# Hybrid decoder step: a state update over 128 rows, one product for all new keys, small loads and cache copies in program order

## The chip, the cores and the metric

The kernel runs on one core of a Trainium2 chip. The metric is the device time of one execution in microseconds (us); lower is better. Three runs of the kernel before gave a median of 3202.14 us (3200.97 to 3202.41). On TensorE's clock the profile prints the granted share: 1.00 is 2.4 GHz and 0.50 is 1.2 GHz.

## What is computed

One step of a one-layer decoder trunk for two groups: a prompt of 2048 tokens, and 8 sample sequences of 8 new tokens each, with a cache of 128 keys and values and a recurrent state. The reference, cut to what matters here:

```python
def layer_forward(x, pos, cache_k, cache_v, conv_state, ssm_state, p, decode):
    proj = rms_norm(x, p['norm_w']) @ p['w_in']
    q, k, v, z_a, z_s, xbc, dt_raw, g = jnp.split(proj, [...], axis=-1)
    if decode:      # k_all, v_all: 128 cached and 8 new positions of each sequence
        o_a, new_k, new_v = window_attention_decode(q, k, v, cache_k, cache_v, p['sinks'])
    else:
        o_a = window_attention_prompt(q, k, v, p['sinks'])
    o_s, new_conv, new_ssm = ssd_branch(xbc, z_s, dt_raw, conv_state, ssm_state, p, chunk)
    merged = jax.nn.sigmoid(g_a) * ((o_a * jax.nn.silu(z_a)) @ p['w_attn_proj']) \
           + jax.nn.sigmoid(g_s) * (o_s @ p['w_ssd_proj'])
    return x + merged @ p['w_out'], new_k, new_v, new_conv, new_ssm

# window_attention_decode returns, beside the attention, the last 128 rows of [cache ; new]
#   (120 cached rows and 8 new ones) as the new window
# ssd_scan:  states = einsum('bclgn,bclgh,bclghp->bcghpn', B, decay_to_end * dt, x)
#            h      = h * chunk_decay + states
```

Everything is f32. Model width 1024, 16 query and 4 key heads of 64, 32 state heads of 64 by 128 in 4 groups.

## The kernel before

Three phases share one core. **T1** (`phase_t1`, line 376) takes the prompt in four blocks of 512 tokens: for each block 256 columns of `w_in` at a time are loaded (`raw`, two buffers, line 154), split into a rounded high part and a rest (`whl`, two buffers, lines 149 to 151: ScalarE casts, VectorE subtracts), and multiplied on TensorE (lines 171 and 195). Each block runs the z_attn tiles (`za_tile`), the keys, the values, the queries and the windowed attention. While a block runs, the next block's `xt` rows are loaded and normed (`prep_h`, line 286). **S** (`phase_s`, line 718) projects x, B, C and z of the recurrent branch and scans the state, four blocks by four groups. **T2** (`phase_t2`, line 1139) does the gates and the output products, block 3 first; the two sample phases, `phase_sa` (attention, line 608) and `phase_ss` (state, line 939), are called inside the first block of T2, and their instructions are interleaved with the products of the prompt.

What sets the order: every DMA of the kernel is issued by one engine, SP, in one queue, and every engine runs its instructions in the order in which they stand. That order is made when the program is built, by a scheduler that takes instructions as soon as its own model of time has them ready, so a load that depends on nothing may be put far ahead of the place where the program text has it.

The places that the change touches:

- `init3` (line 227): loads of small tables for phases S and T2. `sinkS` is 16 loads of 8 times 4 bytes; `Dcol` is two loads, each 64 partitions by 16 elements of 4 bytes that lie 8 bytes apart in memory (line 244 and 246). The text calls `init3` at block 3 of T1 (line 586).
- `phase_sa`, lines 641 to 644: the copies of 120 of 128 cached rows of each sequence to the output windows, one DMA of 960 KB for keys and one for values, from memory to memory.
- `phase_sa`, lines 654 to 690, a loop over the 8 sequences. The probabilities `ss` (128 rows of head and token, 136 positions) are transposed in two pieces, 128 positions (line 679) and 8 (line 680); `po` takes two products per key head: 128 cached values (line 689) and the sequence's own 8 new values `vn` (line 690).
- `phase_ss`, lines 1068 to 1097: the state update `st` of four sequences by two heads. `wxs` holds a rounded part in partitions 0 to 63 and its rest in 64 to 127; `Beh` is the rounded B for all 128 rows, `Bel` the rest of B for the first 64.

```python
PE.matmul(pst_, wxs[:, i * P : (i + 1) * P], Beh, start=True, stop=False)
PE.matmul(pst_, wxs[:64, i * P : (i + 1) * P], Bel, start=False, stop=True)
```

Of the kernel before, what the change touches and what calls it, by code (L numbers as in the profile page):

```python
# [17 lines left out]
P = 128  # L18
# [60 lines left out]
def build(tc, nc, a, o, seq, phases=("T1", "S", "T2"), dbg=None):  # L79
# [146 lines left out]

    def init3(xp, trp):
        rows = xp.tile([P, 2, P], F32, name="rows3", tag="xt")
        SY.dma_start(rows[:96, 0], a["conv_w"][0].rearrange("k (c p) -> (k c) p", p=P))
        SY.dma_start(rows[96:120, 0], a["conv_b"][0].rearrange("(c p) -> c p", p=P))  # L230
        SY.dma_start(rows[:16, 1], a["ssd_norm_w"][0].rearrange("(c p) -> c p", p=P))
        ips = trp.tile([P, 256], F32, name="tr", tag="tr")
        PE.transpose(ips[:, :120], rows[:120, 0], ident[:120, :120])
        PE.transpose(ips[:, 128:144], rows[:16, 1], ident[:16, :16])
        V.tensor_scalar(cwb.rearrange("p k c -> p (k c)"), ips[:, :120], 0.5, None, ALU.mult)
        V.tensor_copy(snw, ips[:, 128:144])
        for h in range(NH):
            SY.dma_start(sinkS[8 * h : 8 * h + 8], a["sinks"][0][h : h + 1].partition_broadcast(8))
        V.tensor_scalar(nsinkS, sinkS, -1.0, None, ALU.mult)
        SY.dma_start(A_bc, a["A_log"][0].partition_broadcast(P))  # L240
        A.activation(A_bc, A_bc, AF.Exp)
        V.tensor_scalar(A_bc, A_bc, -1.0, None, ALU.mult)
        SY.dma_start(dtb_bc, a["dt_bias"][0].partition_broadcast(P))
        dv = a["D_skip"][0].rearrange("(c l) -> l c", l=2)
        for hl in range(2):
            SY.dma_start(Dcol[64 * hl : 64 * hl + 64], dv[hl].partition_broadcast(64))
# [361 lines left out]
    def phase_sa(oas):  # L608
        with ExitStack() as es:
# [43 lines left out]
            po = op.tile([P, 2, 8, 32], F32, name="po", tag="po")  # L653
            for b in range(8):
# [3 lines left out]
                vn = wk.tile([8, 256], F32, name="vn", tag="vn")  # L658
                SY.dma_start(vn, vn_d[8 * b : 8 * b + 8])
# [17 lines left out]
                softmax(wk, s, mx, 136, nsinkS, sinkS, 1)  # L677
                tr = trp.tile([P, 256], F32, name="tr", tag="tr")
                PE.transpose(tr[:, :P], s[:, 0, :P], ident)
                PE.transpose(tr[:8, P:], s[:, 0, P:], ident)  # L680
                PT = wk.tile([P, P], F32, name="PTs", tag="PTs")
                PTn = wk.tile([8, P], F32, name="PTn", tag="PTn")
                A.copy(PT, tr[:, :P])
                A.copy(PTn, tr[:8, P:])
                for pair in range(2):
                    for kvl in range(2):
                        kv = 2 * pair + kvl
                        dst = po[64 * kvl : 64 * kvl + 64, pair, b]
                        PE.matmul(dst, cv[:, kv * HD : (kv + 1) * HD], PT[:, kv * 32 : kv * 32 + 32], start=True, stop=False)
                        PE.matmul(dst, vn[:, kv * HD : (kv + 1) * HD], PTn[:, kv * 32 : kv * 32 + 32], start=False, stop=True)  # L690
# [27 lines left out]
    def phase_s():  # L718
        with ExitStack() as es:
# [219 lines left out]
    def phase_ss(vss):  # L939
        with ExitStack() as es:  # L940
# [44 lines left out]
            for g in range(4):  # L985
# [84 lines left out]
                Bl = wk.tile([64, P], F32, name="Bl", tag="Bl")  # L1070
                V.tensor_tensor(Bl, trb[:64], Bh[:64].bitcast(F32), ALU.subtract)
# [3 lines left out]
                for q in range(2):  # L1075
                    bs = slice(4 * q, 4 * q + 4)
                    Beh = wk.tile([P, 4, P], F32R, name="Beh", tag="a")
                    Bel = wk.tile([64, 4, P], F32R, name="Bel", tag="AB")
                    ohb = ohS[:, bs].unsqueeze(2).to_broadcast([P, 4, P])
                    G.tensor_tensor(Beh, Bh.bitcast(F32).unsqueeze(1).to_broadcast([P, 4, P]), ohb, ALU.mult)  # L1080
                    G.tensor_tensor(Bel, Bl.unsqueeze(1).to_broadcast([64, 4, P]), ohb[:64], ALU.mult)
                    for i in range(4):
# [11 lines left out]
                        PE.matmul(pst_, wxs[:64, i * P : (i + 1) * P], Bel, start=False, stop=True)  # L1094
# [234 lines left out]
```

## Time and profile before

| | before |
|---|---|
| median of 3 runs | 3202.14 us (3200.97 to 3202.41) |
| the profiled execution's own time | 3201.39 us |
| its span, first to last instruction | 3199.6 us |
| TensorE products (PE) busy | 3085.4 us, 96% |
| VectorE (DVE) | 2081.5 us, 65% |
| ScalarE (ACT) | 1419.9 us, 44% |
| GpSimd (POOL) | 982.5 us, 31% |
| mean granted TensorE clock | 0.989 |

The profile is one execution, its times are us from the span's start. PE is the products, PEld the loading of weights that runs beside them. A line such as L195 is a line of the kernel before. In rows of single instructions the columns are start, duration, engine and line, operation, output<-inputs, count, and in brackets the idle time of that engine just before, with what ended it. SPq is the SP queue: its duration is how long the issue of a DMA held SP. f32 products are carried out in two passes and show as two instructions; f32r ones (`fp32r` operands) in one.

### The profile page before, as it was taken

How to read it: one execution, taken by the hardware profiler on the slowest of the kernel's cores; microseconds unless marked ns; L12 is line 12 of the kernel's file. 1: busy time of each engine (PE TensorE's matmuls, PEld its weight loads, DVE VectorE, ACT ScalarE, POOL GpSimd, SP SyncE). 2: the span in 40 equal slices, each digit the busy share in tenths (PEclk: the TensorE clock that was granted, in tenths of full speed). 3: DMA queues.
4: the chain of work that ended last, by engine and by line, in shares of the span. 5: the costliest groups of instructions: out<-in, count | busy, mean ns of one | idle time of the engine just before them, and what ended most of it. 6: DMA issues, size and time to landing. Idle time of an engine off the chain costs nothing.

```text
span 3199.6 us, 49248 instructions
## 1 busy us (share of the span) xinstructions
PE 3085.4 (96%) x19038; PEld 2649.2 (83%) x19038; DVE 2081.5 (65%) x3265; ACT 1419.9 (44%) x2786; POOL 982.5 (31%) x905
## 2 busy tenths in 40 slices
PE   6999999998999999999999998999999999999999
PEld 5978787877899877777777776787877799999888
DVE  3877868787777787888878886455555554334433
ACT  3544535455555555555656564333233333222321
POOL 1523232231445555555656664000121100000000
PEclk8999999999999999999999998999999999999999
DMA  6544425333433544444454444445655564345443
GB/s 215 157 141 117 141 76 180 108 107 103 126 121 119 172 130 124 154 148 131 129 167 147 129 141 128 139 131 154 205 181 143 155 206 132 99 132 175 137 107 103
DMA packets 472931, 448.88 MB, mean 140 GB/s; under 512 B 33824, under 2 KB 420664, under 8 KB 472648
## 3 DMA queue, kind: packets, MB, share of 16 engines
q1 hardware_dynamic: 472696, 445.73, 45.2%
q8 instruction: 150, 2.46, 0.3%
q14 instruction: 85, 0.70, 0.1%
HBM read 382.39 MB, written 65.35 MB: 140 GB/s over the span
## 4 chain that ended last, share of the span: by engine, by line
PE 73%; DVE 12%; DMA 5%; POOL 5%; issue 3%; ACT 2%; SPq 0%; POOLq 0%; DVEq 0%; ACTq 0%
PE mm L184 46%; PE mm L195 12%; PE mm L171 5%; DVE acc L760 3%; DVE whl L151 2%; POOL L L857 2%; DMA raw<-in_w_in_dram 2%; PE sc L522 1%; PE tr L551 1%; POOL ws L881 1%; DVE zs L897 1%; PE tr L539 1%; PE st L884 1%; DMA xt<-in_x_prompt_dram 1%; ACT whl L150 1%
## 5 line engine op out<-in xcount | busy, mean ns | idle before, releaser
L184 PE MATMUL mm<-hT,whl 128*128 128x512 f32 (+1 forms) x6720 | 1349.1, 357 | 10.4 <-DMA hT<-h_d 4.1
L184 PEld LDWEIGHTS mm<-hT,whl 128*128 128x128 f32 x6720 | 1119.5, 190 | 181.1 <-issue 12.6
L151 DVE TENSOR_TENSOR whl<-raw,whl 128x2048 fp32r<-128x2048 f32 (+1 forms) x232 | 524.6, 2265 | 280.4 <-ACT whl L150 273.0
L184 PE MATMUL mm<-ot,whl 128*128 128x512 f32 (+1 forms) x2880 | 569.1, 355 | 2.8 <-DVE whl L151 2.5
L184 PEld LDWEIGHTS mm<-ot,whl 128*128 128x128 f32 x2880 | 474.2, 188 | 74.9 <-issue 5.7
L150 ACT CAST whl<-raw 128x2048 fp32r<-128x2048 f32 (+1 forms) x232 | 412.7, 1786 | 263.3 <-PE mm L184 132.5
L195 PE MATMUL mm<-whl,hT 128*128 128x256 f32 (+1 forms) x2304 | 307.8, 289 | 23.7 <-DVE zs L421 17.2
L195 PEld LDWEIGHTS mm<-whl,hT 128*128 128x128 f32 x2304 | 290.7, 192 | 28.2 <-DVE zs L421 17.9
L760 DVE SCALAR_TENSOR_TENSOR acc<-cr,cwb,acc 128x512 f32<-128x512 f32 x288 | 284.5, 990 | 15.8 <-ACT acc L755 7.0
L857 POOL TENSOR_TENSOR L<-L,cbm 128x1024 f32<-128x1024 f32 x64 | 182.5, 2861 | 94.4 <-DVE cbm L846 92.8
L195 PE MATMUL mm<-whl,ot 128*128 128x256 f32 (+1 forms) x1632 | 203.9, 285 | 0.0
L195 PEld LDWEIGHTS mm<-whl,ot 128*128 128x128 f32 (+1 forms) x1632 | 197.6, 188 | 5.3 <-issue 4.9
L171 PE MATMUL mm<-hT,whl 128*128 128x512 f32 x768 | 194.3, 403 | 2.3 <-ACT hT L277 2.1
L855 ACT ACTIVATE L<-AB,acs 128x128 f32<-128x128 f32 x512 | 157.0, 389 | 38.6 <-PE py L878 29.0
L171 PEld LDWEIGHTS mm<-hT,whl 128*128 128x128 f32 x768 | 142.8, 192 | 33.8 <-ACT hT L277 2.5
L368 ACT ACTIVATE s<-s,ng 128x128 f32<-128x128 f32 x256 | 99.9, 393 | 94.4 <-DVE ng L362 84.2
L150 ACT CAST ot<-v 128x512 fp32r<-128x512 f32 x96 | 58.9, 620 | 162.1 <-DVE v L1195 86.9
L881 POOL TENSOR_TENSOR ws<-wx,ws 128x512 fp32r<-128x512 f32 x64 | 112.2, 1752 | 10.1 <-ACT ws L880 9.8
L374 POOL TENSOR_SCALAR s<-s,den 128x128 f32<-128x128 f32 x128 | 50.1, 403 | 202.7 <-DVE den L370 140.6
L826 ACT ACTIVATE th<-mm 128x512 f32<-128x512 f32 (+1 forms) x80 | 40.0, 509 | 160.8 <-PE mm L184 153.6
L764 ACT ACTIVATE th<-acc 128x512 f32<-128x512 f32 x96 | 60.5, 630 | 111.8 <-DVE acc L760 111.7
L1187 ACT ACTIVATE t<-mm 128x512 f32<-128x512 f32 (+1 forms) x76 | 37.6, 518 | 162.4 <-PE mm L184 141.9
(318 smaller groups left out, 3912.5 us busy)
## 6 DMA issues: line engine op xcount, KB each, us to landing
raw<-in_w_in_dram SPq DMA_DIRECT2D x120, 1024.0 KB
hT<-h_d SPq DMA_DIRECT2D x80, 512.0 KB
raw<-in_w_in_dram SPq DMA_DIRECT2D x64, 512.0 KB
AB<-ac_d SPq DMA_DIRECT2D x64, 512.0 KB
raw<-in_w_ssd_proj_dram SPq DMA_DIRECT2D x32, 1024.0 KB
v_d<-zs SPq DMA_DIRECT2D x16, 1024.0 KB
v<-v_d SPq DMA_DIRECT2D x64, 256.0 KB
raw<-in_w_attn_proj_dram SPq DMA_DIRECT2D x64, 256.0 KB
```

What stands on the lines that cost most here:

```text
L150: A.copy(hi, src)
L151: V.tensor_tensor(lo, src, hi.bitcast(F32), ALU.subtract)
L171: PE.matmul(ps, hl[:, x, k, c0 : c0 + P], ht[:, y, :], start=first and i == 0, stop=last and i == n - 1,)
L184: PE.matmul(ps, hl[:, x, k, c0 : c0 + P], ht[:, y, lo : lo + n], start=i == 0, stop=i == 3 * len(hT) - 1,)
L195: PE.matmul(ps, ht[:, x, tt * P : tt * P + m], hl[:, y, k, :n], start=i == 0, stop=i == 3 * len(hT) - 1,)
L368: A.activation(s[:, i, :width], s[:, i, :width], AF.Exp, bias=ng[:, i : i + 1], accum_out=den[:, i : i + 1])
L374: G.tensor_scalar(s[:, i, :width], s[:, i, :width], den[:, i : i + 1], 0.5, ALU.mult, ALU.mult)
L760: V.scalar_tensor_tensor(out=acc, in0=raw[:, k : k + TB], scalar=cwb[:, k, ct : ct + 1], in1=acc, op0=ALU.mult, op1=ALU.add)
L764: A.activation(th, acc, AF.Tanh)
L855: A.activation(L[:, h], AB[:, h], AF.Relu, scale=-1.0, bias=acs[:, hc.start + h : hc.start + h + 1])
L857: G.tensor_tensor(L, L, cbm[:, c].unsqueeze(1).to_broadcast([P, 8, P]), ALU.mult)
L881: G.tensor_tensor(ws[:, 1], wx, ws[:, 0].bitcast(F32), ALU.subtract)
```

## The change

1. `init3`'s loads go through `late`, which pins them to their place in the program's order on SP: after all that the text has before them.
2. The cache copies leave `phase_sa`. They become 16 copies of one sequence each (120 KB), two after every second group of phase S, pinned as well.
3. In `phase_sa` the new values of all sequences are loaded once (`vn`, 64 rows). Each sequence's 8 columns of new probabilities are put into a zeroed tile `new` (128 by 64) on POOL and transposed to 64 rows; `PTn` collects them. The product per sequence and key head is only that with the cache; four products of 64 rows by 256 columns at the end do the new values of all sequences, and are added to a copy of `po`.
4. In `phase_ss` the rest of B (`Bl`) is padded with zeros to 128 rows, `Bel` too, and the second state product runs over 128 rows.

```diff
+    def late(dst, src):
+        tc.keep_in_program_order(SY.dma_start(dst, src))
+
     def init3(xp, trp):
-        SY.dma_start(rows[:96, 0], a["conv_w"][0].rearrange("k (c p) -> (k c) p", p=P))
+        late(rows[:96, 0], a["conv_w"][0].rearrange("k (c p) -> (k c) p", p=P))
...
         for h in range(NH):
-            SY.dma_start(sinkS[8 * h : 8 * h + 8], a["sinks"][0][h : h + 1].partition_broadcast(8))
+            late(sinkS[8 * h : 8 * h + 8], a["sinks"][0][h : h + 1].partition_broadcast(8))
...
-            SY.dma_start(Dcol[64 * hl : 64 * hl + 64], dv[hl].partition_broadcast(64))
+            late(Dcol[64 * hl : 64 * hl + 64], dv[hl].partition_broadcast(64))
...
-                SY.dma_start(ow[:, 0:120], a[f"cache_{nm}"][0].rearrange("b j h d -> b j (h d)")[:, 8:P])
                 SY.dma_start(ow[:, 120:P], scr.rearrange("(b t) c -> b t c", b=8))
...
+            vn = one.tile([64, 256], F32, name="vn")
+            SY.dma_start(vn, vn_d)
+            PTn = one.tile([64, NKV, 8, 32], F32, name="PTn")
             for b in range(8):
...
-                vn = wk.tile([8, 256], F32, name="vn", tag="vn")
-                SY.dma_start(vn, vn_d[8 * b : 8 * b + 8])
...
+                new = wk.tile([P, 64], F32, name="new", tag="new")
+                G.memset(new, 0.0)
+                G.tensor_copy(new[:, 8 * b : 8 * b + 8], s[:, 0, P:136])
                 PE.transpose(tr[:, :P], s[:, 0, :P], ident)
-                PE.transpose(tr[:8, P:], s[:, 0, P:], ident)
+                PE.transpose(tr[:64, P:], new, ident)
...
-                A.copy(PTn, tr[:8, P:])
+                A.copy(PTn[:, :, b], tr[:64, P:].rearrange("p (v q) -> p v q", v=NKV))
...
-                        PE.matmul(dst, cv[:, kv * HD : (kv + 1) * HD], PT[:, kv * 32 : kv * 32 + 32], start=True, stop=False)
-                        PE.matmul(dst, vn[:, kv * HD : (kv + 1) * HD], PTn[:, kv * 32 : kv * 32 + 32], start=False, stop=True)
+                        PE.matmul(dst, cv[:, kv * HD : (kv + 1) * HD], PT[:, kv * 32 : kv * 32 + 32], start=True, stop=True)
+            pon = one.tile([P, 2, 8, 32], F32, name="pon")
+            A.copy(pon, po)
+            pn = op.tile([P, 2, 8, 32], F32, name="po", tag="po")
+            for pair in range(2):
+                for kvl in range(2):
+                    kv = 2 * pair + kvl
+                    PE.matmul(
+                        pn[64 * kvl : 64 * kvl + 64, pair].rearrange("p b q -> p (b q)"), vn[:, kv * HD : (kv + 1) * HD],
+                        PTn[:, kv].rearrange("p b q -> p (b q)"), start=True, stop=True,
+                    )
+            V.tensor_tensor(pon, pn, pon, ALU.add)
+            po = pon
...
                     stats(b, g)
+                    for nm in ("k", "v"):
+                        for r in range((4 * b + g) * 8 // (4 * NB), (4 * b + g + 1) * 8 // (4 * NB)):
+                            late(o[f"{nm}_win_s"][r, 0:120], a[f"cache_{nm}"][0, r, 8:P].rearrange("j h d -> j (h d)"))
...
-                Bl = wk.tile([64, P], F32, name="Bl", tag="Bl")
-                V.tensor_tensor(Bl, trb[:64], Bh[:64].bitcast(F32), ALU.subtract)
+                Bl = wk.tile([P, P], F32, name="Bl", tag="Bl")
+                G.memset(Bl[64:], 0.0)
+                V.tensor_tensor(Bl[:64], trb[:64], Bh[:64].bitcast(F32), ALU.subtract)
...
-                    Bel = wk.tile([64, 4, P], F32R, name="Bel", tag="AB")
+                    Bel = wk.tile([P, 4, P], F32R, name="Bel", tag="AB")
...
-                        PE.matmul(pst_, wxs[:64, i * P : (i + 1) * P], Bel, start=False, stop=True)
+                        PE.matmul(pst_, wxs[:, i * P : (i + 1) * P], Bel, start=False, stop=True)
```

How the change moves instructions is read from the built programs. In the rows below a line number belongs to its own program (the changed kernel's lines are 3 to 20 further down), then comes the operation, output<-inputs and the size of the output, and xN for N in a row.

SP, block 0 of T1, before, from the last stores of the first block's `hT` on (`xt` is the next block's input, `raw` the next weights, `out_dram` the output windows):

```order
L282 DMA h_d_1_61<-hT 128x1024
L238 DMA sinkS<-in_sinks_dram 8x1
L240 DMA A_bc<-in_A_log_dram 128x32
L282 DMA h_d_1_61<-hT 128x1024
L243 DMA dtb_bc<-in_dt_bias_dram 128x32
L246 DMA Dcol<-in_D_skip_dram 64x16x1 x2
L290 DMA xt<-in_x_prompt_dram 128x1024
L282 DMA h_d_1_61<-hT 128x1024
L290 DMA xt<-in_x_prompt_dram 128x1024
L643 DMA out_dram<-in_cache_k_dram 8x2x15360
L282 DMA h_d_1_61<-hT 128x1024
L643 DMA out_dram<-in_cache_v_dram 8x2x15360
```

The same stretch after:

```order
L285 DMA h_d_0_60<-hT 128x1024
L577 DMA tab_2442<-in_rope_p_dram 128x4x80
L285 DMA h_d_1_61<-hT 128x1024 x2
L293 DMA xt<-in_x_prompt_dram 128x1024 x2
L285 DMA h_d_1_61<-hT 128x1024 x2
L157 DMA raw<-in_w_in_dram 128x8x256 x3
L476 DMA dt_d_112<-dtt 128x128
```

All loads of `init3` and both cache copies are gone from between the stores and the loads of `xt` and `raw`.

SP, block 3 of T1, after (before, `dt_d` followed the store of `oa_d` directly; L228 is the line of `late`):

```order
L157 DMA raw<-in_w_in_dram 128x8x256
L566 DMA oa_d_1_73<-zs 128x4x128
L228 DMA rows_6540<-in_conv_w_dram 96x128
L228 DMA rows_6540<-in_conv_b_dram 24x128
L228 DMA rows_6540<-in_ssd_norm_w_dram 16x128
L228 DMA sinkS<-in_sinks_dram 8x1 x16
L228 DMA A_bc<-in_A_log_dram 128x32
L228 DMA dtb_bc<-in_dt_bias_dram 128x32
L228 DMA Dcol<-in_D_skip_dram 64x16x1 x2
L476 DMA dt_d_115<-dtt 128x128
L157 DMA raw<-in_w_in_dram 128x8x128 x6
```

The 23 small loads now stand here, ahead of the weights of the last z_attn tiles.

PE, second sequence of `phase_sa`, before (`mm` are products of the prompt):

```order
L679 MATMUL tr<-cst,ss 128x128
L680 MATMUL tr<-cst,ss 8x128
L663 MATMUL tr<-cst,ck 64x128 x4
L184 MATMUL mm<-ot,whl 128x512 x2
L184 MATMUL mm<-hT,whl 128x512 x17
L689 MATMUL po<-PTs,cv 64x32
L690 MATMUL po<-PTn,vn 64x32
L689 MATMUL po<-PTs,cv 64x32
L690 MATMUL po<-PTn,vn 64x32
L689 MATMUL po<-PTs,cv 64x32
L690 MATMUL po<-PTn,vn 64x32
```

and after:

```order
L685 MATMUL tr<-cst,ss 128x128
L686 MATMUL tr<-cst,new 64x128
L666 MATMUL tr<-cst,ck 64x128 x4
L184 MATMUL mm<-ot,whl 128x512 x2
L184 MATMUL mm<-hT,whl 128x512 x17
L694 MATMUL po<-PTs,cv 64x32 x4
L673 MATMUL sc<-KC,QS 32x128
```

The transposes and the products of the prompt stand as before; the products of 8 rows between those of 128 are gone. In `phase_ss` all 32 products with `Beh` and 32 with `Bel` are still there, and the phase stands later among the prompt's products: its last one (`st<-ones,sq`) has 86 products of 256 columns and 96 of 288 behind it before the first that reads the sample's result, where it had 220 and 96.

## Rows read from the trace of the kernel before

**Rows 1.** The page's table of engines: busy us, share of the span, instructions.

```profile
PE 3085.4 (96%) x19038; PEld 2649.2 (83%) x19038; DVE 2081.5 (65%) x3265; ACT 1419.9 (44%) x2786; POOL 982.5 (31%) x905
```

**Rows 2.** Windows: stretch, us, busy of PE, PEld, DVE, ACT, POOL; PEclk; DMA share; GB/s.

```profile
40.00:60.00 20.00, 9.13 (x62) 8.00 (x60) 3.04 (x4) 0.23 (x1) 0.00 (x0) 0.88 0.14 37
...
60.00:80.00 20.00, 13.66 (x87) 13.66 (x88) 9.94 (x12) 7.49 (x11) 6.58 (x10) 0.69 0.79 303
...
80.00:100.00 20.00, 18.48 (x150) 18.24 (x149) 10.74 (x16) 6.90 (x11) 10.13 (x9) 1.00 0.36 116
...
640.00:660.00 20.00, 20.00 (x172) 20.00 (x170) 15.62 (x29) 9.18 (x22) 9.40 (x9) 1.00 0.29 75
...
2050.00:2100.00 50.00, 50.00 (x269) 41.01 (x268) 29.47 (x54) 17.06 (x28) 0.60 (x1) 1.00 0.45 148
...
2250.00:2300.00 50.00, 47.79 (x371) 42.36 (x370) 23.52 (x51) 13.00 (x17) 11.49 (x8) 1.00 0.74 225
```

**Rows 3.** Timeline, block 0 of T1: SP, ACT, DVE and PE around the long stall.

```profile
40.59 1.44 SPq L246 DMA_DIRECT2D Dcol<-in_D_skip_dram  x2
...
42.13 3.15 SPq L290 DMA_DIRECT2D xt<-in_x_prompt_dram  x1
...
63.94 1.06 ACT L251 ACTIVATE junk<-xt 128x1024 bf16<-128x1024 f32 x1 [20.95 <-DMA xt<-in_x_prompt_dram]
...
65.60 0.69 DVE L421 SCALAR_TENSOR_TENSOR zs<-th,mm 128x512 f32<-128x512 f32 x1 [21.27 <-ACT th L420]
...
66.34 14.12 PE L195 MATMUL mm<-whl,hT 128*128 128x256 f32 x89 [16.10 <-DVE zs L421]
```

**Rows 4.** DMA view of 40 to 62 us, and a 2 us window inside it.

```profile
DMA packets 2620, 1.02 MB, mean 46 GB/s; under 512 B 2383, under 2 KB 2383, under 8 KB 2620
...
56.00:58.00 2.00, 0.00 (x0) 0.00 (x0) 0.00 (x0) 0.00 (x0) 0.00 (x0) 0.50 0.05 0
```

**Rows 5.** Timeline, block 3 of T1: SP, ACT and PE where the small loads now stand.

```profile
619.45 0.32 PE L233 MATMUL tr<-cst,rows 120*128 120x120 f32 x1
...
621.71 0.38 SPq L563 DMA_DIRECT2D oa_d<-zs  x1
...
636.63 1.00 SPq L157 DMA_DIRECT2D raw<-in_w_in_dram  x2
...
659.32 1.99 ACT L150 CAST whl<-raw 128x1024 fp32r<-128x1024 f32 x2
```

**Rows 6.** Timeline, DVE and PE: sample attention, and other products of 64 columns of weights.

```profile
617.58 1.94 PE L551 MATMUL tr<-PT,vT 128*64 128x512 f32 x8
...
2103.05 0.30 PE L689 MATMUL po<-PTs,cv 128*64 128x32 f32 x2
...
2104.88 0.44 PE L670 MATMUL sc<-KC,QS 64*32 64x128 f32 x8
...
2107.02 0.29 DVE L372 TENSOR_SCALAR ss<-ss,den 128x136 f32<-128x136 f32 x1
...
2112.05 0.27 PE L679 MATMUL tr<-cst,ss 128*128 128x128 f32 x1
```

**Rows 7.** Timeline, PE in `phase_ss`: the two state products and what follows them.

```profile
2246.43 0.39 PE L1093 MATMUL st<-Beh,wxs 128*128 128x512 f32 x1
...
2246.75 0.50 PE L1094 MATMUL st<-Bel,wxs 64*128 64x512 f32 x1
...
2247.18 0.51 PE L195 MATMUL mm<-whl,ot 128*128 128x256 f32 x2
...
2265.91 0.39 PE L1093 MATMUL st<-Beh,wxs 128*128 128x512 f32 x1
...
2266.13 1.00 PE L195 MATMUL mm<-whl,ot 128*128 128x256 f32 x7
```

**Rows 8.** Timeline, PE and DVE at the end of `phase_ss`.

```profile
2592.29 0.63 PE L1127 MATMUL st<-ones,sq 128*64 128x1 f32 x8
...
2600.07 2.23 DVE L1137 TENSOR_TENSOR vss<-vss,rb 128x256 f32<-128x256 f32 x4 [3.02 <-DMA rb<-rss_d]
```

More of the change, by code (lines that the diff above doesn't have):

```diff
@@ L225, in init2 @@
         V.tensor_scalar(wrow[:, 0], wrow[:, 0], 0.125, None, ALU.mult)
+    def late(dst, src):
+        tc.keep_in_program_order(SY.dma_start(dst, src))
     def init3(xp, trp):
         rows = xp.tile([P, 2, P], F32, name="rows3", tag="xt")
-        SY.dma_start(rows[:96, 0], a["conv_w"][0].rearrange("k (c p) -> (k c) p", p=P))
-        SY.dma_start(rows[96:120, 0], a["conv_b"][0].rearrange("(c p) -> c p", p=P))
-        SY.dma_start(rows[:16, 1], a["ssd_norm_w"][0].rearrange("(c p) -> c p", p=P))
+        late(rows[:96, 0], a["conv_w"][0].rearrange("k (c p) -> (k c) p", p=P))
+        late(rows[96:120, 0], a["conv_b"][0].rearrange("(c p) -> c p", p=P))
+        late(rows[:16, 1], a["ssd_norm_w"][0].rearrange("(c p) -> c p", p=P))
         ips = trp.tile([P, 256], F32, name="tr", tag="tr")
@@ L237, in init3 @@
         for h in range(NH):
-            SY.dma_start(sinkS[8 * h : 8 * h + 8], a["sinks"][0][h : h + 1].partition_broadcast(8))
+            late(sinkS[8 * h : 8 * h + 8], a["sinks"][0][h : h + 1].partition_broadcast(8))
         V.tensor_scalar(nsinkS, sinkS, -1.0, None, ALU.mult)
-        SY.dma_start(A_bc, a["A_log"][0].partition_broadcast(P))
+        late(A_bc, a["A_log"][0].partition_broadcast(P))
         A.activation(A_bc, A_bc, AF.Exp)
         V.tensor_scalar(A_bc, A_bc, -1.0, None, ALU.mult)
-        SY.dma_start(dtb_bc, a["dt_bias"][0].partition_broadcast(P))
+        late(dtb_bc, a["dt_bias"][0].partition_broadcast(P))
         dv = a["D_skip"][0].rearrange("(c l) -> l c", l=2)
         for hl in range(2):
-            SY.dma_start(Dcol[64 * hl : 64 * hl + 64], dv[hl].partition_broadcast(64))
+            late(Dcol[64 * hl : 64 * hl + 64], dv[hl].partition_broadcast(64))
     def norm_x(xt, jp, nwb, n=P):
@@ L677, in phase_sa @@
                 softmax(wk, s, mx, 136, nsinkS, sinkS, 1)
+                new = wk.tile([P, 64], F32, name="new", tag="new")
+                G.memset(new, 0.0)
+                G.tensor_copy(new[:, 8 * b : 8 * b + 8], s[:, 0, P:136])
                 tr = trp.tile([P, 256], F32, name="tr", tag="tr")
                 PE.transpose(tr[:, :P], s[:, 0, :P], ident)
-                PE.transpose(tr[:8, P:], s[:, 0, P:], ident)
+                PE.transpose(tr[:64, P:], new, ident)
                 PT = wk.tile([P, P], F32, name="PTs", tag="PTs")
-                PTn = wk.tile([8, P], F32, name="PTn", tag="PTn")
                 A.copy(PT, tr[:, :P])
-                A.copy(PTn, tr[:8, P:])
+                A.copy(PTn[:, :, b], tr[:64, P:].rearrange("p (v q) -> p v q", v=NKV))
                 for pair in range(2):
@@ L1077, in phase_ss @@
                     Beh = wk.tile([P, 4, P], F32R, name="Beh", tag="a")
-                    Bel = wk.tile([64, 4, P], F32R, name="Bel", tag="AB")
+                    Bel = wk.tile([P, 4, P], F32R, name="Bel", tag="AB")
                     ohb = ohS[:, bs].unsqueeze(2).to_broadcast([P, 4, P])
                     G.tensor_tensor(Beh, Bh.bitcast(F32).unsqueeze(1).to_broadcast([P, 4, P]), ohb, ALU.mult)
-                    G.tensor_tensor(Bel, Bl.unsqueeze(1).to_broadcast([64, 4, P]), ohb[:64], ALU.mult)
+                    G.tensor_tensor(Bel, Bl.unsqueeze(1).to_broadcast([P, 4, P]), ohb, ALU.mult)
                     for i in range(4):
```

## Prediction

> **What bounds the kernel now.** I read the page's table of engines first. TensorE is busy for 96% of the span, the others for 65% and less [rows 1]. So an edit pays in one of two ways only: it closes one of TensorE's few gaps, or it makes TensorE's own work shorter. The gaps are 114 us in all (span 3199.6 less 3085.4). The windows show where the largest is: from 40 to 100 us PE is idle for 10.87, 6.34 and 1.52 us, together 18.7 us, while 2050 to 2100 has no gap and 2250 to 2300 only 2.2 us [rows 2].
>
> The timeline of 40 to 100 us then says what ended that gap; the reader should follow it backwards. PE waited 16.10 us for the VectorE step on `zs`, which had waited 21.27 us for ScalarE's `th`; ScalarE runs in order and stood at the `junk` of the next block's norm, 20.95 us, for the DMA of `xt` [rows 3]. On SP, the issue of `xt` at 42.13 stands directly behind the two `Dcol` loads, issued at 40.59. What those loads cost is in the DMA view: of the 2620 packets between 40 and 62 us, 2383 are under 512 B, and 2 x 64 x 16 = 2048 of these are `Dcol`'s single elements. In a window inside the stall the DMA share is 0.05, less than one of 16 engines (0.06), at 0 GB/s [rows 4]: one engine works through tiny packets and all else in the queue waits. The wait of ScalarE ends when `xt` lands, 63.94; 42 us to there, less some 2 us for `xt` itself, leaves about 19 us as the length of that stretch, an estimate.
>
> The gap has a second price. The granted clock at 56 to 58 is 0.50, which is the 1.2 GHz level [rows 4], and the mean of 60 to 80 is 0.69 [rows 2]. With only 0.50 and 1.00 in play, 0.5x + 1.0(20 - x) = 0.69 x 20 gives x = 12.4: half clock until about 72.4. PE worked from 66.34 [rows 3], so it ran 6.1 us at half clock, where 3.0 us would have done.
>
> **The change, part by part.** The sum is made against the profiled execution, 3201.39 us; the median of the runs is 0.75 us above it, which I neglect.
>
> *A, loads leave block 0.* The rows of the order on SP show `xt` and `raw` with neither the small loads nor the cache copies ahead. What goes is the wait of 16.1 us and 3.0 us of half clock: **-19.1**. Late next are the `xt` rows and the `raw` weights themselves; with 1.97 MB of copies gone too, which ran at 303 GB/s [rows 2], there is less ahead of them than there was. Bounds: -14 if a new short wait for `xt` stays, -21.7 if the other 2.6 us of gaps in this stretch go too.
>
> *B, sample attention.* Per sequence the 16 passes of `po` run from 2103.05 to 2104.88: 1.83 us, 0.115 each [rows 6]. Half of them are dropped. The nearest row for what is left are the small products of `sc`, which follow each other without a change of rows: 0.44 for 8, 0.055 each [rows 6]; at 0.115 each nothing is saved by ending the alternation itself. I take 0.08, about midway, for each of 8 passes, so 0.64 in place of 1.83, or 1.2 a sequence, 9.6 over eight. Against that stand four products of 64 rows and 256 columns in two passes each, 8 passes. Products of 512 columns take 1.94 for 8 [rows 6], so half, 0.12, for 256: 1.0, and 0.3 for going in and out: **-8.3** (bounds -5.8, with 0.115 kept, and -9.8, with 0.055). The wider transposes of `new` have the same 128 columns to pass and are taken at nothing. POOL's memset and copy come between the softmax's last VectorE step (2107.02, 0.29 long) and the transpose at 2112.05: 4.7 us of room [rows 6]. If they took longer than that, PE would wait in each sequence; the nearest rows are on other engines, so I leave up to 4 us for it in the range.
>
> *C, state update.* The pair of products starts at 2246.43, the 64-row one at 2246.75, the next work at 2247.18: 0.75 us. The 128-row one alone took 0.22 (2265.91 to 2266.13) [rows 7]. So rows changing from 128 to 64 and back costs 0.3 in a pair. Two equal products should take 0.44 to 0.46; I take 0.29 saved, 32 times: **-9.3**, since PE is all but full there (47.79 of 50 [rows 2]) and nothing else takes up the time. Here a rule speaks against the edit. What the rows say is that the pair with 64 rows costs 0.30 us more than two products of 128 rows would. The Trainium skill, in "TensorE: Matmul & The Clock Gate", section "Why this matters for your kernels", has for products over few rows: "K=32 single mm = same time as K=128". By that alone the padding saves nothing and the term is 0, a rival below; this trace does not agree for the mixed pair. Bounds: 0 and -10.
>
> *D, the small loads in block 3.* The order places all 23 behind the store of `oa_d`, issued at 621.71, and ahead of the weights, `raw` x2, issued at 636.63 [rows 5]. The issues take some 0.37 each (`oa_d` 0.38 [rows 5]), 8.5 us, so `Dcol` starts at 630 to 632 on before's clock and holds the one DMA engine for 19 us, to 651 at the latest; with 2 to 4 us of their own the weights land by 655. The cast that needs them ran at 659.32 [rows 5]: 4 to 6 us of room. I cost this at **0**; the cover is the queries and attention of block 3, and without it the stall of A is paid again: up to 19 and 3. `rows` are needed for transposes that ran at 619.45 [rows 5] and now stand 80 products later (some 10 us), by when these short loads are in.
>
> *E, cache copies in phase S.* 16 issues of 0.38 on SP, hidden as SP is not what PE waits for there; 960 KB each for keys and values spread over more than 1000 us. **0** (0 to +5, if loads of S wait behind them).
>
> *F, fillings on POOL and ScalarE.* The memsets of 64 rows, the copy of `po` and the add at the end: POOL is busy 31%, ScalarE 44% [rows 1]. **0** (0 to +3).
>
> *G, the end of the sample's state.* After its last product, at 2592.29, the phase has a chain through DRAM that ends with VectorE's `vss` at 2600.07 and 2.23 [rows 8]: 10 us. Now 86 products of 256 columns at some 0.12 and 96 of 288 at 0.135 (by columns) cover it, 23 us. **0** (0 to +4).
>
> Sum: -19.1 - 8.3 - 9.3 = -36.7, and 3201.4 - 36.7 = 3164.7. I forecast **3165**.
>
> **The rivals.** *The stall only moves.* In block 3 the weights land after ScalarE wants them. For it: the same loads in the same form stand ahead of weights again, and 4 to 6 us of room is thin against a stretch of 19. Against it: from 640 to 660 PE was busy for all of 20 us [rows 2], so weights were in no short supply there. It costs 5 to 15 us (a late cast, partly covered by what PE has queued); with 10 the time is 3175. Chance 0.17.
>
> *Padding buys nothing.* The product of 64 rows is slow for its place, not for its rows: then C is 0 and the time 3174. The rows speak against it: `Beh` alone is followed after 0.22, in the pair after 0.32. Chance 0.06.
>
> *Slower: the state update starves PE.* The phase now stands later among the prompt's products, with fewer left between, and its `st` pairs need copies `Bel` of twice the rows from POOL. If POOL or the loads of the state come too late, PE waits at each pair. The other parts gain 27.4 (A and B), so slower than before begins at 27.4/32 = 0.86 us of wait beyond the 0.75 of before, 1.6 us a pair, and over the bound of 0.2% (6.4 us, about what a measurement of this kernel tells from no change) at 1.06. With 1.2 us of wait a pair: 3201.4 - 27.4 + 38.4 = 3212. For it speaks that the 2.2 us of gaps of 2250 to 2300 lie in this phase [rows 2]; against it, that POOL is busy for 11.49 of those 50 us [rows 2]. Chance 0.03.
>
> That the loads are not moved at all is excluded by the order on SP.
>
> **How the numbers follow.** My forecast has 0.74; the three rivals have 0.17, 0.06 and 0.03. Its own bounds add up as A -14 to -21.7, B -4 (with POOL late -1.8) to -9.8, C -8 to -10, and up to 8 from E, F and G; not all fall the same way, so with all gains at their high ends the time is 3160, and I go 8 further, to 3152, for what moves that I did not cost; the high end of the forecast alone is 3175. The first two rivals reach to 3185 if they come with small losses; **3152 to 3182** takes in most of both and leaves out less than 2 in 10. Faster by over 0.2%: 0.95; within 0.2%: 0.02 (a stall in block 3 of the full length with C at 0); slower: 0.03.
>
> **What would show it.** Right: from 40 to 72 us no half clock and no wait over 2 us; a stretch with the DMA share at 0.05 at about 612 to 631 (block 3 starts earlier by A) with PE busy through it; eight passes of `po` in a row in well under 1 us; `st` pairs 0.45 apart. Wrong: a wait of PE or ScalarE for `raw` in block 3 (D), pairs still at 0.75 (C), a wait of the new transposes for POOL (B), gaps of PE between 2200 and 2650 that were not there, or a wait for `rb` before the third block of the output products (G). The prediction as a whole falls if the half clock appears anywhere it had not been: 3 us then for every 6 us of work.

## The result, and the profile after

The changed kernel takes 3165.31 us in the median of four runs (3161.97 to 3170.36) against 3202.27 us before (four runs, 3200.97 to 3208.05): ratio 0.9882, 95% interval [0.9864, 0.9901], 38 us less (32 to 44). Forecast were 3165, with 3152 to 3182 around it. As the parts below show, that the middle was hit so closely is partly luck: two gains were larger than forecast, and a loss that had been put at nothing took the surplus back, and in the profiled execution more than that.

The profiled execution is the slowest of the four, 3170.36 us with a span of 3168.2; against [rows 1] PE's busy time fell by 21.4 us and the span by 31.4, so some 10 us of idle time went too. The page's table of engines after:

```profile
PE 3064.0 (97%) x18982; PEld 2638.7 (83%) x18982; DVE 2082.5 (66%) x3266; ACT 1421.1 (45%) x2787; POOL 977.8 (31%) x925
```

The windows after, with the columns of [rows 2]: block 0, then the place of the small loads in block 3, then the end of block 3.

```profile
40.00:60.00 20.00, 20.00 (x153) 19.39 (x152) 13.25 (x16) 8.43 (x12) 7.76 (x10) 1.00 0.43 146
60.00:80.00 20.00, 20.00 (x166) 20.00 (x164) 9.56 (x16) 5.78 (x9) 7.50 (x9) 1.00 0.34 109
80.00:100.00 20.00, 20.00 (x173) 20.00 (x171) 15.94 (x31) 10.47 (x20) 8.20 (x9) 1.00 0.21 56
...
610.00:620.00 10.00, 10.00 (x87) 10.00 (x86) 6.54 (x11) 3.89 (x7) 6.52 (x7) 1.00 0.05 4
620.00:630.00 10.00, 10.00 (x87) 10.00 (x87) 7.20 (x12) 5.25 (x8) 6.62 (x7) 1.00 0.05 0
690.00:700.00 10.00, 1.82 (x6) 0.98 (x8) 8.06 (x16) 5.21 (x17) 0.72 (x2) 0.69 1.01 365
```

PE has no gap left from 40 to 100 us, and its clock stays at 1.00, where [rows 2] had 18.7 us idle and 0.88 and 0.69. The stretch with the DMA share of 0.05 is back at 610 to 630, and PE works through it. But 690 to 700 has 8.2 us of idle time, which stood nowhere in the sum. Half clock is not new there: before, the same place had 4.7 us of idle time and a clock of 0.71:

```profile
710.00:720.00 10.00, 5.28 (x29) 4.23 (x26) 9.80 (x17) 5.61 (x14) 3.13 (x2) 0.71 1.02 378
```

The timeline of ACT, DVE and PE there (duration of a row of several is that of all):

```profile
689.00 3.70 ACT L150 CAST whl<-raw 128x2048 fp32r<-128x2048 f32 x2
...
692.74 0.40 ACT L371 ACTIVATE s<-s,ng 128x128 f32<-128x128 f32 x1
...
690.93 4.49 DVE L151 TENSOR_TENSOR whl<-raw,whl 128x2048 fp32r<-128x2048 f32 x2 [0.16 <-ACT whl L150]
...
695.74 0.16 DVE L372 TENSOR_TENSOR den<-den,es 128x4 f32<-128x4 f32 x1
...
696.43 0.61 DVE L375 TENSOR_SCALAR s<-s,den 128x128 f32<-128x128 f32 x2
...
696.86 1.13 PE L542 MATMUL tr<-cst,s 128*128 128x128 f32 x4 [8.30 <-DVE s L375]
```

PE needs the scaled probabilities `s`. Their exps (L371) wait on ScalarE behind two casts of phase S's first weights, 3.7 us, and the scaling waits on VectorE behind the two subtracts of the same weights, 4.5 us. No DMA ends any of these waits. In the order of the program before, ScalarE takes these casts after the exps of that softmax:

```
before:  L368 ACTIVATE s,den<-s,ng 128x128 x3
         L365 ACTIVATE es<-es 128x4
         L368 ACTIVATE s,den<-s,ng 128x128
         L420 ACTIVATE th<-mm 128x512
         L150 CAST hT<-hs 128x64 x2
         L150 CAST whl<-raw 128x2048 x2
after:   L423 ACTIVATE th<-mm 128x512
         L150 CAST hT<-hs 128x64 x2
         L150 CAST whl<-raw 128x2048 x2
         L150 CAST hT<-hs 128x64
         L371 ACTIVATE s,den<-s,ng 128x128 x4
```

That this is built into the order, by a pin on loads of tables, the prediction had not looked for. Before, the same place had a wait of its own, from the same subtracts, but a shorter one:

```profile
716.68 1.12 PE L496 MATMUL tr<-cst,qr 128*128 128x128 f32 x4 [4.72 <-DVE qr L351]
```

The sample phases after, PE's timeline:

```profile
2101.44 0.43 PE L694 MATMUL po<-PTs,cv 128*64 128x32 f32 x8
2101.80 0.44 PE L673 MATMUL sc<-KC,QS 64*32 64x128 f32 x8
...
2170.88 1.08 PE L701 MATMUL po<-PTn,vn 64*64 64x256 f32 x8
2171.89 0.96 PE L184 MATMUL mm<-ot,whl 128*128 128x512 f32 x3
...
2243.83 0.39 PE L1113 MATMUL st<-Beh,wxs 128*128 128x512 f32 x1
2244.06 0.39 PE L1114 MATMUL st<-Bel,wxs 128*128 128x512 f32 x1
2244.29 0.52 PE L195 MATMUL mm<-whl,ot 128*128 128x256 f32 x3
```

Eight passes of `po` take 0.36 us (2101.44 to 2101.80) where 16 took 1.83 [rows 6]; the end product of all sequences takes 1.01 us (2170.88 to 2171.89); the `st` pair takes 0.46 us where it took 0.75 [rows 7]. PE's waits there from 2190 to 2640, by what ended them (total, times, longest), do not name `rb`, `Bel` or POOL; the first is a load of the state (the last row below is the same wait before):

```profile
PE tr L1108 <- DMA h<-in_state_ssm_dram: 4.1, 3, 2.2
PE st L1113 <- DVE h L1116: 1.4, 1, 1.4
...
PE tr L1088 <- DMA h<-in_state_ssm_dram: 0.9, 1, 0.9
```

To see where the time went, the traces are laid side by side at five products that come in every version: the product a sixteenth of the way through T1's `mm<-whl,hT` (83.35 us before), one at 13 sixteenths of it (609.71, early in block 3), the middle one of phase S's `py` (1445.58), T2's first `mm<-ot,whl` (2012.29) and its last `mm<-whl,ot` (3196.14). The table has the change in each stretch against before, from one profiled execution each.

| | block 0 | to block 3 | end of T1 and half of S | rest of S | T2 | all |
|---|---|---|---|---|---|---|
| the change | -22.0 | +0.9 | +10.9 | -1.4 | -19.9 | -31.5 |
| the change again (e5) | -22.4 | -0.5 | +8.7 | +1.5 | -18.4 | -31.0 |
| e1, pinned loads only | -20.1 | -1.7 | +8.0 | +0.5 | +4.5 | -8.9 |
| e2, products only | +0.2 | +2.0 | +3.1 | +0.8 | -8.4 | -2.3 |
| e3, padding only | +1.6 | -0.1 | +2.4 | -1.7 | -9.2 | -7.1 |
| e4, D in 128 packets only | -16.8 | -2.0 | +0.5 | +1.6 | +0.7 | -15.9 |
| e6, change, D in 128 packets | -21.9 | +2.7 | +9.1 | +1.5 | -24.0 | -32.6 |
| e7, change, casts held | -22.8 | -2.3 | +8.9 | +1.8 | -21.1 | -35.4 |
| e8, loads not pinned, D in 128 | -18.7 | +3.1 | -0.7 | +3.8 | -20.3 | -32.9 |
| e9, copies only | -2.6 | 0.0 | +1.2 | -1.1 | +4.1 | +1.5 |
| e10, e6 and e7 together | -22.5 | -2.1 | +2.7 | +2.2 | -14.5 | -34.2 |
| e11, e8 and a later hold | -19.7 | -0.6 | +2.8 | +0.9 | -22.2 | -38.8 |
| e12, D loaded twice | +19.3 | -0.3 | -1.4 | +1.9 | -2.8 | +16.8 |

The second column, where the programs do nearly the same, shows the scatter of one execution: some 3 us to either side. T2 scatters more: the four versions that leave its work alone (e1, e4, e9, e12) have -2.8 to +4.5 there. Runs of one kernel differ by up to 14 us (before, 3199 to 3213 over all chips), so a term of 2 or 3 us is not told from the totals.

### The profile page after: what moved, and what is told of

The parts are those of the page before. It is cut to its first block, busy times and chain, and to the rows that moved or that the text cites. A ratio compares the mean times of both kernels' runs of the same rounds, so it can differ in the third digit from the quotient of the medians.

```text
span 3168.2 us, 49176 instructions
## 1 busy us (share of the span) xinstructions
PE 3064.0 (97%) x18982; PEld 2638.7 (83%) x18982; DVE 2082.5 (66%) x3266; ACT 1421.1 (45%) x2787; POOL 977.8 (31%) x925
## 4 chain that ended last, share of the span: by engine, by line
PE 73%; DVE 13%; POOL 5%; DMA 4%; issue 3%; ACT 2%; SPq 0%; POOLq 0%; DVEq 0%; ACTq 0%
PE mm L184 46%; PE mm L195 12%; PE mm L171 5%; DVE acc L776 3%; DVE whl L151 2%; POOL L L873 2%; PE tr L554 2%; PE sc L525 1%; POOL ws L897 1%; DVE zs L913 1%; PE tr L542 1%; DMA raw<-in_w_in_dram 1%; PE st L900 1%; PE py L894 1%; DMA v<-v_d 1%
## 5 line engine op out<-in xcount | busy, mean ns | idle before, releaser
L371 ACT ACTIVATE s<-s,ng 128x128 f32<-128x128 f32 x256 | 99.9, 393 | 88.4 <-DVE ng L365 81.2
L1215 DVE SCALAR_TENSOR_TENSOR v<-v,snw,rb 128x512 f32<-128x512 f32 x64 | 48.1, 767 | 96.0 <-DMA v<-v_d 95.6
```

Source lines behind the costliest of these rows:

```text
L371: A.activation(s[:, i, :width], s[:, i, :width], AF.Exp, bias=ng[:, i : i + 1], accum_out=den[:, i : i + 1])
```

## The experiments

The first four take the change apart.

**e1, the pinned loads alone**, part 1 of the diff: `init3` uses `late`; the cache copies and all products are before's.

> Only part 1: the loads of init3 are pinned, the cache copies stay in phase_sa, products as before. Theory: this part alone gives -22 us in block 0 (stall and half clock gone) and gives back about 10 us at the end of block 3, where its built order, as that of the change, puts casts of phase S's first hT and whl ahead of the last exps of a softmax that PE waits for: about 3202 - 22 + 10 = 3190 us, with a wait of some 8 us at about 690. Rival: the give-back comes from the 16 cache copies in phase S or from the products, then 3180. Second rival: the cache copies, which here still stand ahead of xt in block 0, hold the stall up, then less than 16 of the 22 us are gained.

Measured: 3191.66 us, ratio 0.9956 [0.9941, 0.9970], 14 us less. Block 0 gains 20.1, with 2.3 us of short waits left where the changed kernel has none, and the end of T1 loses 8.0. Its wait there is the same to a hundredth:

```profile
695.50 1.13 PE L542 MATMUL tr<-cst,s 128*128 128x128 f32 x4 [8.30 <-DVE s L375]
```

So the loss belongs to the pinned loads, not to the copies or the products; both rivals fall.

**e2, the products of the sample attention alone**, the diff's lines in `phase_sa` without the copies.

> Only part 3: the new keys of all sequences in one product per key head. Theory: 8 passes of po in 0.36 us in place of 16 in 1.83, eight times (-11.8), and 1.0 us for the end products: -10.8, so 3191 us. Rival: the copies and the add at the end, or the new order of the products, give some of it back: 3194 to 3198. The stall of block 0 stays.

Measured: 3197.41 us, ratio 0.9974 [0.9965, 0.9983], 8 us less (5 to 11). In its trace each sequence takes 0.36 us for `po` as in the changed kernel, which is worth 8 x 1.48 = 11.8 less 1.0; T2 as a whole is 8.4 us shorter. The missing 2.4 lie within the scatter of a stretch, so whether something is given back stays open.

**e3, the padding alone**, part 4 of the diff.

> Only part 4: the second state product over 128 rows. PE's order is the same as before's, so the term stands alone. Theory: a change between 64 and 128 rows costs PE 0.29 us in a pair, 32 pairs: -9.3, so 3193 us, pairs at 0.46 us. Rival: waits for POOL's wider Bel take it back, then pairs with waits ahead and 3198 to 3202.

Measured: 3195.22 us, ratio 0.9969 [0.9957, 0.9981], 10 us less (6 to 14); T2 is 9.2 us shorter, the forecast of 32 x 0.29, though T2 scatters by more than the two agree. The pairs themselves, with the order of PE unchanged:

```profile
2248.40 0.39 PE L1094 MATMUL st<-Beh,wxs 128*128 128x512 f32 x1
2248.63 0.39 PE L1095 MATMUL st<-Bel,wxs 128*128 128x512 f32 x1
2248.86 0.40 PE L195 MATMUL mm<-whl,ot 128*128 128x256 f32 x2
```

The product over 128 rows does twice the work of the one over 64 and takes 0.23 us where that took 0.43 [rows 7]. The rival that padding buys nothing, and the rule of the Trainium skill behind it ("TensorE: Matmul & The Clock Gate", "Why this matters for your kernels"), do not hold where products over 64 and 128 rows take turns. Its page "TensorEngine Tiling (Array Packing)", section "Key Properties", says that a change of tiling mode drains TensorE; the 0.29 us of a pair fit that, but no run here shows that it is the cause.

**e4, what made the stall.** The kernel before, with every load and copy still in block 0, but D comes in the order of memory.

```diff
...
-        dv = a["D_skip"][0].rearrange("(c l) -> l c", l=2)
+        SY.dma_start(Drow.rearrange("p c l -> p (c l)"), a["D_skip"][0].partition_broadcast(P))
         for hl in range(2):
-            SY.dma_start(Dcol[64 * hl : 64 * hl + 64], dv[hl].partition_broadcast(64))
+            G.tensor_copy(Dcol[64 * hl : 64 * hl + 64], Drow[64 * hl : 64 * hl + 64, :, hl])
```

> The kernel before with one edit: D is loaded in the order of memory, 128 packets of 128 bytes, and picked apart by two copies on POOL; the other small loads and the cache copies stay ahead of xt. Theory: the stall of block 0 is made by the 2048 packets of 4 bytes alone, so it goes as in the change: -19 to -22, and the boundary of block 3 stays as before (its casts stand where they stood): 3180 to 3183. Rival: the cache copies (1.97 MB, about 7 us at 303 GB/s) or the 16 loads of sinkS hold xt up as well: then a wait of 5 to 10 us stays and the time is 3187 to 3195.

Measured: 3186.18 us, ratio 0.9946 [0.9931, 0.9962], 17 us less (12 to 22) by the ratio, 19.5 by the medians (3205.69 before on that chip). The wait of 16.1 us is gone, from PE's timeline:

```profile
44.67 11.79 PE L196 MATMUL mm<-whl,hT 128*128 128x256 f32 x97 [2.16 <-DVE zs L422]
...
62.01 3.43 PE L196 MATMUL mm<-whl,hT 128*128 128x288 f32 x24 [1.82 <-DVE qn L335]
66.54 1.73 PE L196 MATMUL mm<-whl,hT 128*128 128x288 f32 x11 [1.09 <-DVE dtt L473]
```

The `xt` loads have no less ahead of them than before: on SP, one of the cache copies even moved in front of the first. The DMA view from 40 to 62 us has 494 packets under 512 B, where [rows 4] has 2383.

```profile
40.65 0.82 SPq L644 DMA_DIRECT2D out_dram<-in_cache_k_dram  x1
41.57 0.37 SPq L291 DMA_DIRECT2D xt<-in_x_prompt_dram  x1
...
DMA packets 2855, 6.37 MB, mean 289 GB/s; under 512 B 494, under 2 KB 2184, under 8 KB 2822
```

One edit to how 32 numbers are fetched gives half of what the whole change gives, without taking a load out of block 0. The waits in PE's rows above, 5.1 us, go in the changed kernel, where the copies have left as well. The end of T1 keeps before's order and loses nothing (+0.5). The Trainium skill, "DMA: Bandwidth & Descriptors", section "Rules for kernel authors", says that a strided last dimension becomes one descriptor per element and should be made contiguous; the trace agrees: 2 x 64 x 16 elements are 2048, and some 1900 small packets went from the view with this edit.

**e12, the dose.** Both loads of D are made twice, the second time into a tile that nothing reads.

```diff
...
             SY.dma_start(Dcol[64 * hl : 64 * hl + 64], dv[hl].partition_broadcast(64))
+            SY.dma_start(Dcol2[64 * hl : 64 * hl + 64], dv[hl].partition_broadcast(64))
```

> The kernel before with the two loads of D made twice (into a second tile that nothing reads), 4096 packets of 4 bytes. By the packet theory the stretch with one busy DMA engine grows from 19 to some 38 us; the first xt stands behind two of the four loads as before, the second xt behind three, the weights (raw) behind all: PE's wait in block 0 grows from 16 us to between 25 and 40, and the time by 10 to 25 us. By a rival in which the wait is set by the number of queue entries ahead, not by their packets, it grows by less than 3 us.

Measured: 3220.93 us, ratio 1.0043 [1.0028, 1.0058], 14 us more; block 0 is 19.3 us longer in the trace. The first wait is as before, and a second of 19 us has come, for the weights, which stand behind the other 2048 packets. The rows are of PE, of ScalarE, and of the windows:

```profile
68.65 13.57 PE L196 MATMUL mm<-whl,hT 128*128 128x256 f32 x89 [16.15 <-DVE zs L423]
...
102.64 3.73 PE L196 MATMUL mm<-whl,hT 128*128 128x288 f32 x14 [19.06 <-DVE dtt L474]
...
98.27 1.90 ACT L151 CAST whl<-raw 128x2048 fp32r<-128x2048 f32 x1 [20.86 <-DMA raw<-in_w_in_dram]
...
90.00:92.00 2.00, 0.00 (x0) 0.00 (x0) 0.00 (x0) 0.00 (x0) 0.00 (x0) 0.50 0.50 208
```

Both waits together, 35 us, lie within the 25 to 40 expected; the second `xt`, though, stood behind two of the four loads on SP, not three. The price is in the packets, and the rival of queue entries falls. The second wait is not packets from end to end: at 90 to 92 us DMA moves 208 GB/s, which are transfers that had been held up. The price of a packet is read where nothing else moves, in the kernel before from 46 to 56 us:

```profile
DMA packets 1078, 0.00 MB, mean 0 GB/s; under 512 B 1078, under 2 KB 1078, under 8 KB 1078
```

That is 9.3 ns for each, 19.0 us for 2048, and block 0 grew by 19.3.

**e9, the cache copies alone**, as in the diff.

> Only part 2: the cache copies go from block 0 into phase S, the small loads stay ahead of xt. Theory: the stall of block 0 is the packets of D, so it stays, and 16 copies of 120 KB in phase S cost nothing that shows: the time of the kernel before, within 4 us. Rival: the copies slow the loads of phase S, or their absence from block 0 shortens what follows the stall: more than 4 us off to either side.

Measured: 3201.01 us against 3206.38, ratio 0.9985 [0.9975, 0.9995], 5 us less (2 to 8), which does not decide between the theory and the rival, whose line was at 4. Block 0's wait is 15.18 us in place of 16.1, and the stretch 2.6 us shorter, which agrees with the 2.3 us of waits that e1 kept; phase S shows nothing beyond the scatter (+1.2 and -1.1). The copies had a small part in block 0, and cost nothing that can be seen where they stand now.

The four parts together, e1, e2, e3 and e9: 14 + 8 + 10 + 5 = 37 us, each known to 3 to 5 us, and the whole change 38. They add up within that, and the loss at the end of T1 lies inside the 14.

The rest asks what the loss at the end of T1 is.

**e5, the change again**, beside e6 to e8 on one chip.

> The changed kernel once more, beside the three below on one chip: 3165 us, with the wait of 8.3 us at about 689 and no stall in block 0.

Measured: 3170.82 us against 3208.54, ratio 0.9881 [0.9863, 0.9898]; the wait of 8.30 us at 695 is there again.

**e6, the change with D in 128 packets**, e4's edit with `late` for the load; PE's order is not touched.

> The changed kernel with D loaded in 128 packets of 128 bytes, in the same place; PE's order is the same. Theory: the stretch of one busy DMA engine in block 3 (some 19 us) was hidden, and the 8.3 us at the end of block 3 are a matter of the order of the casts: same time as the changed kernel within 2 us, the wait of 8.3 stays. Rival: the stretch holds the weights or hT back and so makes the wait: 5 to 10 us faster and the wait gone.

Measured: 3166.25 us, ratio 0.9873 [0.9857, 0.9889], not to be told from the change. The long wait stays:

```profile
696.76 1.13 PE L543 MATMUL tr<-cst,s 128*128 128x128 f32 x4 [8.30 <-DVE s L376]
```

So the DMA stretch in block 3 does not make it. What does go is a smaller wait: the changed kernel has one of 1.54 us at 636, at the end of the stretch, e5 and e1 of 1.54 and 1.42, e7 of 2.38; e6 and e10, without the tiny packets, have none.

**e7, the change with the casts held.**

```diff
...
+        if cur.get("hold", 0):
+            cur["hold"] -= 1
+            tc.add_manual_dep(
+                got.ins, cur["exps"][-9].ins.name,
+                mybir.DependencyInfo(mybir.DependencyClass.Sync, mybir.DependencyReason.DATA),
+                reason="first weights of S behind a softmax",
+            )
```

`got` is the cast in `wload`, for the first two weights of phase S, and the dependency puts it behind the last exp of the softmax that it had passed (the ninth from the end).

> The changed kernel with one dependency more: the first two casts of phase S's weights stand behind the last exp of the softmax that they had passed. Theory: PE's 8.3 us wait and the half clock behind it go, 5 to 10 us faster than the changed kernel: 3156 to 3160. Rival: the casts are only late somewhere else (as before's own order, which lost 4.7 us there): the gain is 0 to 4 us.

Measured: 3164.67 us, ratio 0.9871 [0.9853, 0.9889], 6 us below e5, but the intervals overlap. PE's timeline at the two places:

```profile
632.90 0.98 PE L203 MATMUL mm<-whl,hT 128*128 128x256 f32 x6 [2.38 <-issue]
...
690.24 1.14 PE L551 MATMUL tr<-cst,s 128*128 128x128 f32 x4 [3.57 <-DVE s L384]
692.69 3.42 PE L563 MATMUL tr<-PT,vT 128*64 128x512 f32 x8 [1.32 <-DVE PT L553]
...
699.61 0.80 PE L534 MATMUL sc<-KTT,qT 128*128 128x256 f32 x2 [2.47 <-DVE qT L514]
```

The casts do make the wait: held back, 8.30 becomes 3.57. But 2.47 us come back at the queries, whose own casts now stand behind those of the weights, and this stretch of the table is no shorter (+8.9, where e5 on the same chip has +8.7). From the early block 3 to phase S, PE's idle time falls only from 26.5 to 24.2 us, and its work at half clock rises from 20.3 to 23.3. The rival was right that the casts are late somewhere else; the theory had counted the whole wait as gain.

**e8, the loads not pinned**, but D in 128 packets, and parts 2 to 4 of the change.

> Parts 2 to 4 of the change, but the small loads are not pinned: they stay in block 0, with D in 128 packets. Theory: block 0 gains about 22 as in the change (the copies are gone from there too), the end of block 3 stays in the order of before and gives nothing back, the products gain 20: 3202 - 42 = 3160, some 5 to 8 us faster than the changed kernel. Rival: the other 20 small loads still cost a wait in block 0, then 3163 to 3167, as the changed kernel.

Measured: 3168.74 us, ratio 0.9879 [0.9860, 0.9897], 39 us less (33 to 45) than before on the same chip, where the theory had 42 and the change again has 38 (e5). The two are not told apart, so the 5 to 8 us over the change are not shown. The end of T1 is as forecast, before's order of casts and no loss (-0.7). What it lacks against the theory lies elsewhere: block 0 gains 18.7, with PE 1.9 us idle from 40 to 80 us where the change has nothing, and the table's other stretches of T1 and S lose 3.1 and 3.8, the size of the scatter of one execution. The rest stays open.

**e10, e6 and e7 together.**

> The changed kernel with both edits: D in 128 packets and the first weights of phase S behind the softmax. The waits of 1.5 to 2.4 us for weights in block 3 that the changed kernel and the one with the held casts had should go, as with D in 128 packets alone, and the 8.3 us be cut to about 3.6: 5 to 8 us faster than the changed kernel, ratio to before 0.9855 to 0.987. If the two edits only move waits about, the ratio stays at 0.988.

Measured: 3166.18 us, ratio 0.9868 [0.9853, 0.9883]. As expected the wait at 636 is gone and the long one is 3.57; the stretch loses 2.7 where the change loses 8.7 to 10.9. But T2 gains only 14.5, with 13.1 us of PE idle in it where e7, whose PE and ScalarE orders are the same, has 8.1: T2 scatters too. The ratio is no proof of a gain.

**e11, e8 with a later hold**: the same dependency, one softmax further on (the eighth from the end).

> The kernel with parts 2 to 4, D in 128 packets in block 0 and, new, the first weights of phase S held behind one more softmax. If the casts ahead of the queries' rotation make the 4.7 us wait that this order has at the end of block 3, that wait goes and the time falls by up to 4.7 us and some half clock against the run without the hold: ratio to before 0.986. If the products that need these weights are what fills PE there, the time rises instead, 0.988 to 0.99.

Measured: 3162.84 us (3162.09 to 3163.98), ratio 0.9862 [0.9848, 0.9875], the lowest of all. The wait for the queries' rotation is 1.28 us where e8 has 4.72, but others have come, the longest 2.22, and the stretch is no shorter than e8's (+2.8). So the gain has not the place that was expected. Its interval and those of the change (0.9864 to 0.9901, 0.9863 to 0.9898) overlap: it is not shown to beat the changed kernel.

## Why the prediction was right, point by point

*A, loads leave block 0.* Forecast -19.1, measured -22.0, just past the bound of -21.7. The reading was right: e4 and e12 show that the 2048 packets of `Dcol` set the wait; at the 9.3 ns of a packet they take 19.0 us, the 19 that were estimated, and 2048 more made block 0 19.3 us longer. The term was 2.9 us too small because the other short gaps in the stretch were left standing; they went, since the cache copies left too (2.3 to 2.6 us by e1 and e9). In one point the wording went too far: the rows show packets one after the other at the share of one engine, not that it is one engine.

*B, sample attention.* Forecast -8.3, by the trace 11.8 - 1.0 = -10.8, by e2's runs -8 (5 to 11). The mis-sized step is the price of a pass: 0.08 was taken between 0.055 and 0.115, and it is 0.355 / 8 = 0.044, below the end that the row of `sc` gave. The end products were sized well (1.3 against 1.0). POOL's memset and copy fit into the slack: from 2050 to 2180 PE waits 0.3 us in all, for weights.

*C, state update.* Forecast -9.3; the pairs fell from 0.75 to 0.46, 32 x 0.29 = 9.3, and T2 in e3 by 9.2, closer than its scatter lets one expect. The row of a lone 128-row product was the right price for the padded one.

*D, the small loads in block 3.* Put at 0, it is +8 to +11, and this step failed. The argument was about landing times, and those held: weights land in time, PE is busy through the stretch, and all that the packets cost is a wait of 1.5 us. What it left out is the order on ScalarE and VectorE. The step compared SP's and PE's orders, and the program's scheduler had in the same build moved two casts and two subtracts ahead of a softmax that PE waits for. The four profiles with the loads pinned and the casts not held lose 8.0 to 10.9 in that stretch of the table, and the six that keep before's order of these casts -1.4 to +3.1. PE's idle time from the early block 3 to phase S separates them more clearly: 20.0 us before and 19.9 to 20.7 in the six (e2, e3, e4, e8, e9, e12), 24.8 to 26.9 in the four (the change, e5, e1, e6). The windows of before and of the changed kernel, and PE's waits in them that differ most (total, times, longest; first before, then after):

```profile
609.71:821.46 211.75, 191.72 (x1307) 167.13 (x1305) 160.98 (x357) 102.91 (x294) 59.70 (x80) 0.95 0.33 101
588.61:810.49 221.88, 194.94 (x1306) 166.98 (x1305) 159.93 (x359) 103.76 (x295) 59.85 (x80) 0.95 0.33 96
...
PE tr L496 <- DVE qr L351: 4.7, 1, 4.7
PE tr L539 <- DVE s L372: 2.9, 2, 2.4
...
PE tr L542 <- DVE s L375: 11.2, 3, 8.3
PE mm L195 <- issue: 1.5, 1, 1.5
PE tr L499 <- DVE qr L354: 0.2, 1, 0.2
```

So 8.3 us of new waits for `s` stand against 4.5 less at the queries' rotation, and 1.5 of the "issue" wait and smaller ones make up the 6.9 us. The two casts alone are not all of it: holding them gave back 2.3 us of idle time (e7 against e5) and 2.6 (e10 against e6). How much half clock adds is not shown: the changed kernel has 19.1 us of work at half clock there against 15.9, but the six have 15.3 to 19.5. The rival *The stall only moves* had the place, and with 5 to 15 us the size, but late weights, its mechanism, are not what happened.

*E, F, G* held. E's 16 copies do not show in phase S, and their leaving block 0 was part of A. POOL and ScalarE hide F. For G, `vss` is done at 2590 and PE waits for nothing of it. The rival *Slower* needed waits of about 1 us at each of 32 pairs; PE's waits from 2190 to 2640 are nine, 7.5 us in all. Before they were five, 4.4 us: 3 us of new gaps, nearly all for loads of the state (4.1 in place of 0.9), had been put at nothing, and they are one of the signs that the prediction gave for being wrong.

Sum: forecast -19.1 - 8.3 - 9.3 + 0 = -36.7, in the trace -22.0 - 10.8 - 9.3 + 10.9 = -31.2, against the 31.4 by which the span fell; B and C stand here as their own rows give them, and T2 as a whole fell by 19.9. In the medians the change is worth 37 us, since the profiled execution was the slowest of its four: the same forecast is 5 us off against one and right against the other. One slip in the range: it takes B's low end as -4, where the term itself has -5.8; with that the forecast's own high end is 3174 and not 3175, which changes nothing.

## What to carry to other kernels

A load that fetches single elements is paid for by whatever stands behind it in its queue: count packets, not bytes, and change the access first, as e4 did, before changing the order. Where a scheduler makes the order, a pin on one queue can move work on every engine: compare the orders of all engines that feed the bottleneck, not only of the one that is pinned. And products over 64 rows between products over 128 cost more than zeros do.

## What the runs showed of the hardware that was not expected

Small products gain more from standing together than the nearest rows said: 0.115 us a pass in turn with 8-row products, 0.044 in a row. And with 2048 packets of 4 bytes in flight PE waited 1.4 to 2.4 us "for issue", a wait for which the view names no engine and no DMA, at the end of the stretch (four profiles of four with the packets in block 3, none of the two with 128 packets); no run was made to find what it waited for. The DMA view points at loads of instructions. In the changed kernel, q8, one of the queues that the view marks as instruction, brings nothing from 607 to 634 us, while the small packets pass, and one packet from 634 to 637; PE goes on at 636.3. In e6, where D comes in 128 packets, q8 brings two from 609 to 636, and PE has no such wait. The rows are PE's wait and, from these windows, the queues (packets, MB, share); from 607 to 634 q1 is the only one:

```profile
636.31 0.98 PE L195 MATMUL mm<-whl,hT 128*128 128x256 f32 x6 [1.54 <-issue]
...
q1 hardware_dynamic: 2858, 0.21, 6.6%
...
q8 instruction: 1, 0.02, 2.0%
...
q8 instruction: 2, 0.03, 0.6%
```

That the packets held this queue up, and PE with it, fits all four profiles; no experiment shows it.
